# Joined small inputs, an earlier bias, another staging slot and two orders of ScalarE work in a streaming-encoder kernel

## The chip, the cores and the metric

The kernel runs on one core of a Trainium2 chip. The metric is the device time of one execution in microseconds (us). A core has TensorE (PE, whose weight loads are shown as PEld), VectorE (DVE), ScalarE (ACT), GpSimd (POOL) and SyncE (SP). Each engine works through its own queue in order. Transfers are issued from the queues of SP, POOL and ACT and carried out by 16 DMA engines that all queues share.

## The reference

The reference is one step of a two-layer encoder on 1024 prompt frames and 8 streams of 16 sample frames, width 1024, 16 query heads and 4 key/value heads of 64.

```python
# layer 0 (A): windowed attention with ALiBi distances and a learned sink per head
qkv = rmsnorm(x, g_attn[0]) @ w_qkv_a[0]
q = rmsnorm(q, g_q_a[0]); k = rmsnorm(k, g_k_a[0])
x = x + attend(q, k, v, alibi_bias, sink_a[0]) @ w_o_a[0]
x = x + square(relu(rmsnorm(x, g_mlp[0]) @ w_up[0])) @ w_down[0]
# between the layers: shared keys and values
kv = rmsnorm(x, g_kv) @ w_kv;  k = rmsnorm(k, g_k_b)
# layer 1 (B): the last 9 chunks, learned bias on the clipped distance
q = rmsnorm(rmsnorm(x, g_attn[1]) @ w_q_b[0], g_q_b[0])
x = x + attend(q, k, v, relpos_bias(rel_bias_b[0]), None) @ w_o_b[0]
x = x + square(relu(rmsnorm(x, g_mlp[1]) @ w_up[1])) @ w_down[1]
```

The frames are held as nine tiles of 128: eight of the prompt and one, called ST, of all samples.

## The kernel before

Every matmul operand in 32 bits is split into a high part (a cast on ACT, line 128; for scaled attention weights POOL line 185) and a low part (a subtraction on DVE, line 134 or 190), and a product is three matmuls: high by high, high by low, low by high (lines 219 to 221 in `proj`, 745 to 747 in `mm3`).

The stages follow each other: layer 0 attention (about 0 to 400 us), the rest of its output projection (`wo_phase`, to about 442), its up projection (`mlp_up`, to about 798), its down projection (`mlp_down`, to about 1134), and the same four for layer 1.

**Start.** `prep_gains` loads five gain vectors of 1024 with five SP transfers, turns them in one transpose and keeps them as columns. Then come the first token tile, the key/value weights, two more token tiles, and the vectors g_k, g_q (`load_gvec`, line 627), the constants, and the sink in one transfer for all partitions and four for the sample layout (`sinks`, lines 1349 to 1358). `N(t)` makes a token tile ready: `transpose_x` turns it on PE (line 212) and splits it into `hh` and `hl`; `stats` squares it on ACT (line 203) for the norm. `K1` and `Q1` are the key/value and query projections. SP issues in order, so a load that waits for a free buffer holds what stands behind it.

**Up projection.** Sixteen blocks of 256 columns. Each block loads weights on SP (`ru`, line 773), splits them on DVE and ACT and writes squared activations into two tiles of a seven-tile rotation `h`; every second block takes a third. DVE forms sums of them, and POOL stores them to DRAM as `hd` (line 910). A tile of the rotation is free again when its last store has landed.

**Down projection.** Forty items, grouped in chains that add into the same PSUM banks. Item n needs a block `a` of `hd` (loaded on SP into one of three slots, cast on ACT, low part on DVE) and a weight sum `s` or raw weight `r` (added on DVE at line 1062, cast to slot `w0` or `w1` in turn, low part on DVE). After an item, its three banks are copied out (line 1165 ACT to `o` or a token tile, line 1173) or added to a token tile on DVE (line 1177), and POOL transfers add them to DRAM (`xp`/`xd`). The last outputs of layer 0 go, by an ACT copy, into the token tiles x8, x0, x1, from there by line 1168 to DRAM. `DOWN_HOME` is the order of the tiles in memory; layer 1's attention then lays its own tiles over the same addresses, and a tile waits until what lay there before has been read.

**The bias of layer 1's samples.** In the down projection of layer 0, from item 20, `prep_bias` loads the table, fills two tiles on DVE, builds a row per head, and spreads it in DRAM (`rd`, 3 MB); from item 24, `spread_bias` issues sixteen small SP transfers into `big` and one from there to `biasSd`. Their places on DVE and SP are ordered by hand with `behind`.

**Order.** The program order is a priority; a planner with its own estimates of durations fixes each engine's order. `behind(a, b)` puts b after a on the same engine. `chain` orders DVE work in the down projection by hand.

Of the kernel before, what the change touches and what calls it, by code (L numbers as in the profile page):

```python
# [63 lines left out]
C_W = 596  # L64


def shape_constants():
    c = np.zeros((P, C_W), np.float32)
# [19 lines left out]
    return c  # L88

# [5 lines left out]
class Build:  # L95
# [104 lines left out]
    def stats(self, small, junk, x, t):  # L200
        nc = self.nc
        ssq = small.tile([P, 1], F32, tag="xssq", name="xssq")
        nc.scalar.activation(junk, x, AF.Square, accum_out=ssq)
        nc.vector.tensor_scalar(self.vx[:, t : t + 1], ssq, 1.0 / D, EPS, ALU.mult, ALU.add)

    def transpose_x(self, x, hh, hl):
        nc = self.nc
        for half in range(2):
# [4 lines left out]
            self.split(hh[half], hl[half], ps)  # L213
# [753 lines left out]
    def mlp_down(self, layer, out):  # L967
# [3 lines left out]
        with ExitStack() as st:  # L971
# [15 lines left out]
            for n, tags in enumerate(DOWN_HOME):  # L987
                pool = self.pool(st, f"d{n}_{layer}")
                for t in tags.split():
                    if t == "bias":  # L990
                        self.bias_tiles(pool)
                        pool.tile([P, 248], F32, tag="pad", name="pad")
                    elif t[0] == "+":
# [132 lines left out]
            for n, (s, p, g, first, final, reads, _) in enumerate(seq):  # L1126
                if layer == 0 and n == RANK:
                    self.prep_bias(self.dp)
                if layer == 0 and n == RANK + 4:
                    self.spread_bias(self.dp)  # L1130
# [20 lines left out]
                for i in range(3):  # L1151
# [11 lines left out]
                    for o, v in reads:  # L1163
                        if o in adds:
                            nc.scalar.activation(adds[o][i], banks[i], AF.Copy, scale=float(v))  # L1165
# [27 lines left out]
    def bias_tiles(self, pool):  # L1193
        self.tb = pool.tile([H, NREL], F32, tag="tb", name="tb")
        self.fr = pool.tile([H, 384], F32, tag="fr", name="fr")
        self.big = pool.tile([P, KV, 288], F32, tag="big", name="big")

    def prep_bias(self, dp):
        nc = self.nc
        with ExitStack() as st:  # L1200
            tb, fr, big = self.tb, self.fr, self.big
            a = nc.sync.dma_start(tb, self.ins["rel_bias_b"][0])
            self.behind(self.sp, a)
            self.behind(self.dve, nc.vector.memset(fr, 0.0))
            self.behind(self.dve, nc.vector.memset(big, BIG))
            nc.vector.tensor_scalar(
                fr[:, 127:383], tb[:, 256:0:-1], -1.0, tb[:, 256:257], ALU.mult, ALU.add
            )
            fd = dp.tile([H, 384], F32, tag="fd", name="fd")
            nc.sync.dma_start(fd, fr)  # L1210
            rd = dp.tile([H, P, 384], F32, tag="rd", name="rd")
            nc.sync.dma_start(rd, fd[0:H].unsqueeze(1).to_broadcast([H, P, 384]))
            ra = rd[0:H]

            def fsrc(h, off, n, nh, hs, w):
                return bass.AP(
                    tensor=ra.tensor, offset=ra.offset + h * P * 384 + 127 + off,
                    ap=[[383, n], [hs * P * 384, nh], [1, w]],
                )

            self.fsrc = fsrc

    def spread_bias(self, dp):
        nc, big, fsrc = self.nc, self.big, self.fsrc
        for h4 in range(G):
            for b in range(2):
                r = slice(h4 * 32 + b * 16, h4 * 32 + b * 16 + 16)
                c = 256 + b * 16
                for z in (
                    nc.sync.dma_start(big[r, :, b * P : b * P + P], fsrc(h4, 0, 16, KV, G, P)),  # L1230
# [681 lines left out]
```

## Time and profile before

| | us |
|---|---|
| median of 3 runs | 2354.36 (2354.15 to 2357.34) |
| span of the profiled execution | 2349.6 |
| median less span: what lies around it | 4.8 |
| PE busy | 2273.2 |
| DVE busy | 1718.3 |
| ACT busy | 1332.0 |
| POOL busy | 644.7 |

The span runs from the first to the last instruction of one profiled execution; its own time is that span and what lies around it, for which the page has no row; against the median it is 4.8 us. In the timeline a row gives start, length, engine, line, operation, output and inputs, and in square brackets how long the engine was idle before it and what ended the idle time. A row with "x8" merges eight instructions. The mean granted clock of TensorE is 0.993.

### The profile page before, as it was taken

The page shows a single profiled execution, that of the slowest core. Times are in us where ns is not written, and L with a number is a line of the kernel's source. Part 1 is how long each engine was busy: PE and PEld are TensorE (multiplying, and loading weights), DVE is VectorE, ACT ScalarE, POOL GpSimd, SP SyncE. Part 2 cuts the span into 40 slices and gives each one's busy share as a digit, 9 for nine tenths or more (in the row PEclk, how much of TensorE's full clock was granted, in tenths as well). Part 3 has the DMA queues.
Part 4 walks back from the last instruction along what each step waited for, and adds up shares of the span by engine and source line. Part 5 has one row for each costly group of instructions (what it writes and reads, how often), then busy time and mean ns, then how long its engine had stood idle before and what let it go on. Part 6 is the DMA issues. An engine that isn't in the chain of part 4 may idle for free.

```text
span 2349.6 us, 33397 instructions
## 1 busy us (share of the span) xinstructions
PE 2273.2 (97%) x11429; PEld 1899.3 (81%) x11429; DVE 1718.3 (73%) x3075; ACT 1332.0 (57%) x2684; POOL 644.7 (27%) x950
## 2 busy tenths in 40 slices
PE   8999999899999999999899899999899999999999
PEld 6787877788888888778778778887888888888887
DVE  6888786766656578898577776877666566678987
ACT  3777674555555555344377666665655555555443
POOL 4434332313213111002433444345132132210011
PEclk9999999999999999999999999999999999999999
DMA  7435546234334687848654656555243343877567
GB/s 262 128 103 177 166 141 208 89 122 162 132 112 152 218 231 174 272 142 206 191 157 114 190 151 180 166 172 186 72 162 132 114 160 113 276 212 197 183 165 198
DMA packets 226715, 392.70 MB, mean 167 GB/s; under 512 B 51592, under 2 KB 126288, under 8 KB 226448
## 3 DMA queue, kind: packets, MB, share of 16 engines
q1 hardware_dynamic: 188816, 283.58, 37.8%
q0 software_dynamic: 36432, 102.26, 16.0%
q10 hardware_dynamic: 1296, 4.72, 0.5%
q8 instruction: 90, 1.47, 0.3%
q14 instruction: 81, 0.66, 0.1%
HBM read 236.51 MB, written 156.85 MB: 167 GB/s over the span
## 4 chain that ended last, share of the span: by engine, by line
PE 73%; DVE 11%; DMA 8%; ACT 3%; issue 2%; POOL 2%; SPq 1%; ACTq 0%; DVEq 0%; POOLq 0%
PE ps_c L745 7%; PE ps_c L746 7%; PE ps_c L747 7%; PE ps_x L745 5%; PE ps_x L747 5%; PE ps_x L746 5%; PE ps_mm L219 3%; PE ps_mm L221 3%; PE ps_mm L220 3%; PE ps_y L747 2%; PE ps_y L746 2%; PE ps_y L745 2%; PE ps_tr L326 2%; DMA a<-hd 2%; DVE w L134 1%
## 5 line engine op out<-in xcount | busy, mean ns | idle before, releaser
L746 PE MATMUL ps_c<-w,a 128*128 128x512 f32 x960 | 374.0, 390 | 3.9 <-DVE w L134 3.9
L745 PE MATMUL ps_c<-w,a 128*128 128x512 f32 x960 | 374.1, 390 | 3.2 <-ACT o L1165 1.7
L747 PE MATMUL ps_c<-w,a 128*128 128x512 f32 x960 | 373.5, 389 | 0.0
L910 POOL DMA_DIRECT2D hd<-h x272 | 149.4, 552 | 594.3 <-ACT h L819 378.4
L745 PEld LDWEIGHTS ps_c<-w,a 128*128 128x128 f32 x960 | 180.2, 188 | 42.9 <-issue 2.7
L746 PEld LDWEIGHTS ps_c<-w,a 128*128 128x128 f32 x960 | 180.2, 188 | 42.7 <-DVE w L134 5.6
L747 PEld LDWEIGHTS ps_c<-w,a 128*128 128x128 f32 x960 | 180.2, 188 | 37.4
L128 ACT CAST a<-a 128x1536 fp32r<-128x1536 f32 x80 | 118.6, 1483 | 154.6 <-DMA a<-hd 154.6
L219 PE MATMUL ps_mm<-w,hh 128*128 128x512 f32 x432 | 173.9, 403 | 12.8 <-ACT hh L128 5.4
L221 PE MATMUL ps_mm<-w,hl 128*128 128x512 f32 x432 | 172.4, 399 | 1.4 <-DVE hl L134 1.2
L220 PE MATMUL ps_mm<-w,hh 128*128 128x512 f32 x432 | 171.4, 397 | 0.3
L134 DVE TENSOR_TENSOR a<-a 128x1536 fp32r<-128x1536 f32 x80 | 140.6, 1757 | 40.6 <-ACT a L128 40.5
L745 PE MATMUL ps_x<-sx,w 128*128 128x512 f32 (+1 forms) x408 | 157.8, 387 | 4.5 <-ACT h L866 2.7
L128 ACT CAST w<-ru 128x512 fp32r<-128x512 f32 (+1 forms) x160 | 109.9, 708 | 84.4 <-PE ps_y L746 32.0
L128 ACT CAST w<-s 128x2048 fp32r<-128x2048 f32 x56 | 107.1, 1912 | 88.2 <-DVE s L1062 78.8
L747 PE MATMUL ps_x<-sx,w 128*128 128x512 f32 (+1 forms) x408 | 154.2, 378 | 0.3 <-DVE w L134 0.3
L746 PE MATMUL ps_x<-sx,w 128*128 128x512 f32 (+1 forms) x408 | 154.1, 378 | 0.0
L134 DVE TENSOR_TENSOR w<-s,w 128x2048 fp32r<-128x2048 f32 x56 | 128.2, 2289 | 32.3 <-ACT w L128 32.0
L1182 POOL DMA_DIRECT2D xp<-o x28 | 36.2, 1294 | 411.6 <-ACT o L1165 391.0
L134 DVE TENSOR_TENSOR w<-ru,w 128x512 fp32r<-128x512 f32 (+1 forms) x160 | 129.7, 813 | 14.8 <-ACT w L128 14.7
L134 DVE TENSOR_TENSOR ptl<-ps_tr,pth 128x512 fp32r<-128x512 f32 x180 | 122.5, 685 | 21.2 <-ACT pth L128 17.5
L818 ACT ACTIVATE h<-h 128x512 f32<-128x512 f32 (+1 forms) x102 | 61.9, 607 | 122.1 <-DVE h L868 93.0
(274 smaller groups left out, 6152.9 us busy)
## 6 DMA issues: line engine op xcount, KB each, us to landing
a<-hd SPq DMA_DIRECT2D x80, 768.0 KB, 6.2
hd<-h POOLq DMA_DIRECT2D x272, 192.0 KB, 2.5
ru<-in_w_up SPq DMA_DIRECT2D x64, 512.0 KB, 3.9
r<-in_w_down SPq DMA_DIRECT2D x32, 1024.0 KB, 9.8
xp<-o POOLq DMA_DIRECT2D x28, 768.0 KB, 9.5
o<-oTd SPq DMA_DIRECT2D x50, 256.0 KB, 3.9
x<-xp SPq DMA_DIRECT2D x23, 512.0 KB, 5.5
xp<-xo SPq DMA_DIRECT2D x18, 512.0 KB, 2.9
```

The source lines that it names most:

```text
L128: a = nc.scalar.copy(hi, src)
L134: return a, e.tensor_tensor(lo, src, hi.bitcast(F32), ALU.subtract)
L219: nc.tensor.matmul(ps, a, w[:, 0, k, :], start=(k == 0), stop=False)
L220: nc.tensor.matmul(ps, a, w[:, 1, k, :], start=False, stop=False)
L221: self.lp = nc.tensor.matmul(ps, b, w[:, 0, k, :], start=False, stop=(k == KC - 1))
L326: self.lp = nc.tensor.transpose(pt[:, i, :], get(i), self.ident)
L745: a = mm(ps, ah, bh, start=first, stop=False, skip_group_check=True)
L746: mm(ps, ah, bl, start=False, stop=False, skip_group_check=True)
L747: return a, mm(ps, al, bh, start=False, stop=last, skip_group_check=True)
L818: a = nc.scalar.activation(t, src, AF.Relu)
L910: return lambda p, z: self.nc.gpsimd.dma_start(self.hd[c // 4][:, p, c % 4], z)
L1182: nc.gpsimd.dma_start(dst, z, accum_op=ALU.add)
```

## The change

Four edits. (1) The host lays the sinks, g_k and g_q behind the constants in one array of 744 columns and the five gains in one array, so that one transfer loads each; -0.125 is multiplied into g_q in place. (2) The bias preparation moves to the first block of layer 0's up projection. Its tiles are the first two of the seven-tile rotation; its DMAs go to POOL's queue (table, row, sixteen spreads, store), all but the 3 MB spread in DRAM, which stays on SP; no order by hand is given. The addresses that its tiles had in the down projection become a gap. (3) In the last item of a down projection, sums that go straight to DRAM are copied to the weight slot that no later item uses. Only layer 0 has such sums in its last item. (4) In layer 1's attention the square of tiles 0, 1 and ST is ordered behind the casts of that tile, and in both down projections the cast of `a` for item 2 behind the latest copy at line 1165.

```diff
     def stats(self, small, junk, x, t):
-        nc.scalar.activation(junk, x, AF.Square, accum_out=ssq)
+        z = nc.scalar.activation(junk, x, AF.Square, accum_out=ssq)
...
+        return z
...
                 quad, ws = weights(b)
+                if layer == 0 and b == 0:
+                    part, big = [hp.tile([P, 3 * 3 * P], F32, tag="h", name="hb", bufs=7) for _ in range(2)]
+                    self.spread_bias(self.dp, part, big)
...
-                low[n] = [self.split(a[:, 0], a[:, 1], a[:, 1].bitcast(F32))[1]]
+                z = self.split(a[:, 0], a[:, 1], a[:, 1].bitcast(F32))
+                if n == 2:
+                    self.behind(self.copied, z[0])
+                low[n] = [z[1]]
...
-                if layer == 0 and n == RANK:
-                    self.prep_bias(self.dp)
-                if layer == 0 and n == RANK + 4:
-                    self.spread_bias(self.dp)
...
-                            adds[o] = [xs[t][:, N[o % 2]] for t in PARTS[2]]
+                            if n + 1 < total:
+                                adds[o] = [xs[t][:, N[o % 2]] for t in PARTS[2]]
+                            else:
+                                z = take(f"w{(n + 1) % 2}")
+                                adds[o] = [z[:, 0, i].bitcast(F32) for i in range(3)]
                             continue
...
+    def spread_bias(self, dp, part, big):
+        dma = nc.gpsimd.dma_start
+        tb, fr = part[0:H, 0:NREL], part[0:H, 384:768]
+        dma(tb, self.ins["rel_bias_b"][0])
+        nc.vector.memset(fr, 0.0)
+        nc.vector.memset(big, BIG)
+        nc.vector.tensor_scalar(
+            fr[:, 127:383], tb[:, 256:0:-1], -1.0, tb[:, 256:257], ALU.mult, ALU.add
+        )
+        dma(fd, fr)
+        nc.sync.dma_start(rd, fd[0:H].unsqueeze(1).to_broadcast([H, P, 384]))
...
+                dma(big[r, :, b * P : b * P + P], fsrc(h4, 0, 16, KV, G, P))
+                dma(big[r, :, c : c + 16], fsrc(h4, P, 16, KV, G, 16))
+        dma(self.biasSd[0:KV].rearrange("j p c -> p j c"), big)
...
-            for i, v in enumerate(
-                (I["g_attn"][0], I["g_attn"][1], I["g_mlp"][0], I["g_mlp"][1], I["g_kv"])
-            ):
-                nc.sync.dma_start(g[i * KC : (i + 1) * KC, :], v.rearrange("(k p) -> k p", p=P))
+            nc.sync.dma_start(g, I["gains"])
...
-        nc.sync.dma_start(self.sink, I["sink_a"][0].partition_broadcast(P))
+        self.sink = self.cst[:, C_SK : C_SK + H]
...
-        for i in range(G):
-            nc.sync.dma_start(
-                self.ssink[i * 32 : i * 32 + 32, :],
-                sk[i : i + 13 : 4].partition_broadcast(32),
-            )
+        self.ssink = self.cst[:, C_SSK : C_SSK + KV]
...
-                self.transpose_x(x, hh, hl)
-                self.stats(small, self.scratch([P, D], mybir.dt.bfloat16, "junk"), x, t)
+                turned = self.transpose_x(x, hh, hl)
+                z = self.stats(small, self.scratch([P, D], mybir.dt.bfloat16, "junk"), x, t)
+                if not A and t in (0, 1, ST):
+                    self.behind(turned, z)
...
+            if A:
+                self.cst = ring.tile([P, C_W], F32, tag="cst", name="cst")
+                nc.sync.dma_start(self.cst, I["consts"])
+                gk, gq8 = self.cst[:, C_GK : C_GK + HD], self.cst[:, C_GQ : C_GQ + HD]
+                nc.vector.tensor_scalar(gq8, gq8, -0.125, None, ALU.mult)
```

More of the change, by code (lines that the diff above doesn't have):

```diff
@@ L63 @@
 C_SLS = 592
-C_W = 596
+C_SK = 596
+C_SSK = 612
+C_GK = 616
+C_GQ = 680
+C_W = 744
+C_S = 596
 def shape_constants():
-    c = np.zeros((P, C_W), np.float32)
+    c = np.zeros((P, C_S), np.float32)
     q = np.arange(P)[:, None]
@@ L88, in shape_constants, with laid_out @@
     return c
+def laid_out(sink, g_k, g_q):
+    row = np.concatenate([g_k, g_q])
+    return np.concatenate(
+        [
+            shape_constants(),
+            np.broadcast_to(sink, (P, H)),
+            np.repeat(sink.reshape(KV, G).T, P // G, axis=0),
+            np.broadcast_to(row, (P, 2 * HD)),
+        ],
+        axis=1,
+    )
 def halves(t):
@@ L989, in mlp_down @@
                 for t in tags.split():
[L990 to L993, printed above, removed]
+                    if t[0] == "+":
                         pool.tile([P, int(t[1:])], F32, tag="gap", name="gap")
@@ L1164, in mlp_down @@
                         if o in adds:
-                            nc.scalar.activation(adds[o][i], banks[i], AF.Copy, scale=float(v))
+                            self.copied = nc.scalar.activation(
+                                adds[o][i], banks[i], AF.Copy, scale=float(v)
+                            )
                             if o not in whole:
@@ L1396, in attention @@
             ring = self.pool(st, f"ring{layer}")
-            self.pad(st, f"ringpad{layer}", 168 if A else 64)
+            self.pad(st, f"ringpad{layer}", 176 if A else 64)
             apool = self.pool(st, f"att{layer}", 2)
@@ L1875 @@
 ]
+_LAID = ("g_attn", "g_kv", "sink_a", "g_k_a", "g_q_a")
 _OUTS = [
@@ L1896 @@
     given = {n: np.ascontiguousarray(inputs[n]) for n in _INS}
-    given["consts"] = shape_constants()
+    given["consts"] = laid_out(given["sink_a"][0], given["g_k_a"][0], given["g_q_a"][0])
+    given["gains"] = np.concatenate(
+        [given["g_attn"], given["g_mlp"], given["g_kv"][None]]
+    ).reshape(5 * KC, P)
+    for name in _LAID:
+        del given[name]
     given["eye"] = np.eye(P, dtype=np.float32)
```

58 lines of the change are left out of this document (16 added, 42 removed).

## The prediction

> **What bounds the kernel now.** I read the page first, then the chain of waits that ended last, then the waits of PE stage by stage, and last the timelines of all engines around each wait that the change touches.
>
> ```profile
> span 2349.6 us, 33397 instructions
> ...
> PE 2273.2 (97%) x11429; PEld 1899.3 (81%) x11429; DVE 1718.3 (73%) x3075; ACT 1332.0 (57%) x2684; POOL 644.7 (27%) x950
> ```
>
> PE is the bound and the stages stand in series, so an edit is worth the PE idle time that it ends, and 2349.6 - 2273.2 = 76 us of idle time is all there is to win. No edit adds or removes a matmul. The sum is made against the span of 2349.6; the median is 4.8 us more, which I keep as it is.
>
> **Start of layer 0 (edit 1).** Timeline of the first 27 us, SP first, then the engines behind it; the second fence is a row of the chain of waits.
>
> ```profile
> 1.17 0.70 SPq L1246 DMA_DIRECT2D g<-in_g_attn  x2
> ...
> 2.92 0.36 SPq L1426 DMA_DIRECT2D x<-in_x_prompt  x1
> ...
> 9.24 0.33 SPq L1426 DMA_DIRECT2D x<-in_x_sample  x1
> ...
> 10.51 4.38 SPq L1358 DMA_DIRECT2D ssink<-in_sink_a  x4
> ...
> 11.00 0.81 DVE L190 SCALAR_TENSOR_TENSOR w<-raw,gcol,w 128x512 fp32r<-128x512 f32 x1
> ...
> 16.12 0.39 SPq L146 DMA_DIRECT2D raw<-in_w_qkv_a  x1
> ...
> 26.78 0.50 PE L221 MATMUL ps_mm<-w,hl 128*128 128x512 f32 x1 [1.21 <-DVE hl L134]
> ```
> ```profile
> 6.49 9.57 DMA gq<-in_g_q_a
> ```
>
> Five gain loads stand between 1.17 and 2.92, 0.35 us each. Four go, so the first token tile and everything behind it on SP comes 4 x 0.35 = 1.4 us earlier. Of the eight small loads (gk, gq, constants, sink, four ssink) one is left. Today they cost SP 4.38 us for the sinks alone, and the first query weight (16.12) waits until gq has landed, although its buffer was free at 11.0 + 0.81 = 11.8. Afterwards it can go at about 11.8 - 1.4 = 10.4, 5.7 us sooner. PE feels only the last wait: the low part of tile ST stood on DVE behind the low parts of these late weights, 1.21 us. With the weights 5.7 us early that wait goes. Sum 1.4 + 1.2 = **2.6 us**; bounds 0 (the shift ends in a later wait) and 5.7 (the whole advance of the weights).
>
> **Bias moved into the up stage (edit 2).** First what it leaves behind. PE's waits in the middle of the down stage, layer 0, then the same items of layer 1, which has no bias to prepare:
>
> ```profile
> 972.85 0.50 PE L746 MATMUL ps_c<-w,a 128*128 128x512 f32 x1 [1.06 <-DVE w L134]
> 989.75 0.47 PE L745 MATMUL ps_c<-w,a 128*128 128x512 f32 x1 [0.52 <-DVE x L1177]
> ...
> 1000.16 0.50 PE L746 MATMUL ps_c<-w,a 128*128 128x512 f32 x1 [1.74 <-DVE w L134]
> 1017.68 0.50 PE L746 MATMUL ps_c<-w,a 128*128 128x512 f32 x1 [0.91 <-DVE w L134]
> 1034.58 0.47 PE L745 MATMUL ps_c<-w,a 128*128 128x512 f32 x1 [0.51 <-DVE x L1177]
> ```
> ```profile
> 2189.84 0.50 PE L746 MATMUL ps_c<-w,a 128*128 128x512 f32 x1 [0.22 <-DVE w L134]
> 2206.73 0.47 PE L745 MATMUL ps_c<-w,a 128*128 128x512 f32 x1 [0.50 <-DVE x L1177]
> ```
>
> Layer 0 loses 1.06 + 0.52 + 1.74 + 0.91 + 0.51 = 4.74 us, layer 1 0.72. Layer 1 is layer 0 without the bias, so the removal is worth 4.74 - 0.72 = **4.0 us**; bounds 1.06 (only the wait behind the fills of DVE) and 4.74.
>
> Now what it adds. DVE operations and DMAs of the bias, as they are today:
>
> ```profile
> 967.40 0.38 DVE L1204 MEMSET fr<- 16x384 f32 x1
> 967.97 1.02 DVE L1205 MEMSET big<- 128x1152 f32 x1 [0.19 <-issue]
> ...
> 974.92 0.34 DVE L1206 TENSOR_SCALAR fr<-tb 16x256 f32<-16x256 f32 x1
> ```
> ```profile
> rd<-fd SPq DMA_DIRECT2D x1, 3072.0 KB, 15.7
> ...
> biasSd<-big SPq DMA_DIRECT2D x1, 576.0 KB, 5.0
> big<-rd SPq DMA_DIRECT2D x8, 32.0 KB, 5.2
> ...
> fd<-fr SPq DMA_DIRECT2D x1, 24.0 KB, 1.5
> ```
>
> And the place they go to, around the first blocks of the up stage: DVE, POOL, then a stretch (length; busy time and count of PE, PEld, DVE, ACT, POOL; clock; share of the DMA engines; GB/s), and last a group of the page:
>
> ```profile
> 449.20 0.42 DVE L877 TENSOR_TENSOR h<-ps_y,h 128x256 f32<-128x256 f32 x1 [3.99 <-PE ps_y L747]
> ...
> 493.36 0.68 DVE L868 TENSOR_TENSOR h<-ps_z,h 128x512 f32<-128x512 f32 x1
> ```
> ```profile
> 493.74 0.54 POOL L910 DMA_DIRECT2D hd<-ht  x1
> ```
> ```profile
> 446.00:464.00 18.00, 18.00 (x150) 18.00 (x151) 6.31 (x11) 9.90 (x26) 0.60 (x1) 1.00 0.01 1
> ```
> ```profile
> L1182 POOL DMA_DIRECT2D xp<-o x28 | 36.2, 1294 | 411.6 <-ACT o L1165 391.0
> ```
>
> DVE's 0.38 + 1.02 + 0.34 = 1.74 us fit into its idle 3.99 us ahead of 449.2: cost 0. Without that cover, put between the last low parts of the output projection, they would cost their 1.74. In 446 to 464 PE was busy for all of 18.00 us, DVE for 6.31, POOL for 0.60 and the DMA engines for 1%, so this is the emptiest stretch for 3 MB. The chain of the bias: the row is ready at about 445, its store lands by 447.5 (issue 0.54, landing 1.5), the 3 MB by 463 (15.7, measured under full load), sixteen spreads on POOL at 0.54 to 1.29 each by 472 to 484, their landing 5.2 and the store to `biasSd` 5.0 by 483 to 495. Who waits for that: the two bias tiles are the first two of the rotation and come round in block 2, whose second product is added at 493.36; its first copy stands 1.7 us ahead of that and the first write of the second tile, `big`, about 1.1 us behind, at some 494.5. So even the dear end only touches it: cost **0**, bound -1.7. Behind the spreads on POOL stand the first `hd` stores (from 463 on); they end some 10 to 20 us later, and their tiles are wanted in block 3, 22 us after block 2. On SP the weight loads of the next blocks stand behind the 3 MB issue, which waits until the row has landed (447.5); those weights are first cast at 458.
>
> [...]
>
> **First copies of the down stage (edit 4, second half).** Layer 0, then layer 1:
>
> ```profile
> 807.88 0.50 PE L745 MATMUL ps_c<-w,a 128*128 128x512 f32 x1 [1.38 <-ACT o L1165]
> ```
> ```profile
> 2025.85 0.50 PE L745 MATMUL ps_c<-w,a 128*128 128x512 f32 x1 [0.28 <-ACT o L1165]
> ```
>
> Item 1 adds into banks that must first be copied, and the copies stood on ACT behind the cast of `a` for item 2. Put ahead of it, they end with item 0's matmuls: 1.38 + 0.28 = **1.7 us**. The cast is then late by three copies, but item 2 starts a whole item (8 us) later. Bounds 0 and 1.7.
>
> **From layer 0 to layer 1 (edits 3 and 4).** ACT, POOL, PE and SP here:
>
> ```profile
> 1132.16 1.06 ACT L203 ACTIVATE junk<-x 128x1024 bf16<-128x1024 f32 x1 [1.35 <-DMA x<-xp]
> ...
> 1140.13 1.07 ACT L128 CAST hh<-ps_n 128x512 fp32r<-128x512 f32 x2 [5.84 <-DMA xp<-x]
> ```
> ```profile
> 1134.16 1.77 POOL L1168 DMA_DIRECT2D xp<-x  x2
> ```
> ```profile
> 1134.34 1.09 PE L212 MATMUL ps_n<-identr,x 128*128 128x128 f32 x8 [0.67 <-ACT x L1165]
> 1140.86 0.76 PE L219 MATMUL ps_mm<-w,hh 128*128 128x512 f32 x1 [5.43 <-ACT hh L128]
> ...
> 1145.42 0.40 PE L221 MATMUL ps_mm<-w,hl 128*128 128x512 f32 x1
> 1145.66 0.40 PE L219 MATMUL ps_mm<-w,hh 128*128 128x512 f32 x1
> ```
> ```profile
> 1133.74 0.38 SPq L146 DMA_DIRECT2D raw<-in_w_q_b  x1
> ```
>
> This is the largest term. The cast of `hh` does not wait for data: it waits for the transfer `xp<-x` that reads the last sums from token tiles lying at the addresses of `hh`. With the sums in slot w0, far from `hh`, the cast can follow the transposes, and PE's 5.43 us go. The 0.67 us go too: the square at 1132.16 stood ahead of the last copies. There is a third part: eleven matmuls fill 1140.86 to 1145.42, 0.41 us each, against 0.24 after (1145.42 to 1145.66), so the wait also cost 11 x 0.17 = 1.9 us of slow matmuls. [...] Together 5.43 + 0.67 + 1.9 = 8.0 us.
>
> Against it stands a new wait. The first query weight (1133.74) lands in the buffer of token tile 0, which the square must have read. That square now follows the casts: ACT ends its copies at about 1133.4, two casts make it 1134.5, square and read-out 1.25 more, so the load goes at 1135.8, 2.1 us later than today, while PE wants it 8 us sooner. I take those 2.1 us off: **5.9 us**; bounds 0 (the weights give the pace) and 8.0.
>
> **Sum.** 2.6 + 4.0 + 1.7 + 5.9 = 14.2 us. Span 2335.4, time 2354.4 - 14.2 = **2340.2 us**.
>
> **The rivals.**
>
> *The query weights take over.* What the transition wins is lost again at layer 1's first query projection, whose weights pass through two buffers. For it speaks the later first load, against it that SP, too, was held by the stalled cast. Then 2.6 + 4.0 + 1.7 = 8.3 and 2346.1 us.
>
> *The bias was not what held the down stage.* DVE is full in that stretch, and the waits move to other sums. For it: two of five waits end with `x L1177`, which layer 1 has as well. Against it: layer 1's 0.72. Then 14.2 - 4.0 = 10.2 and 2344.2 us.
>
> *Slower: POOL cannot clear the spreads before block 2.* Place: the copy into `big`, at 494.5. If each spread costs not 0.54 to 1.29 but a landing of 5.2 us, sixteen take 83, `big` is free at 463 + 83 + 5 = 551, and PE stands for 56 us: 2340.2 + 56 = 2396 us. It decides from the spread at which the stall eats the 14.2: 463 + 16 s + 10.2 = 494.5 + 14.2, s = 2.2 us. Against it: no POOL issue in the groups is that dear.
>
> *It does not do what it says.* The order of all else comes from the planner, which is fed with changed loads at the start and may give a few us away in either attention stage; if it gives away most of the sum, 2351 or more.
>
> **Chances.** Forecast 0.56; query weights 0.18; bias 0.14; nothing measurable 0.07; slower 0.05. A measurement of this kernel tells 0.2% (4.7 us) from no change: faster is below 2349.7. Faster 0.88, same 0.07, slower 0.05. The range: 2334, from the upper bounds (5.7 + 4.74 + 1.7 + 8.0 = 20.1), to 2350, the lower bounds of two of the large terms at once.
>
> **What would show it.** First query load near 10.4 and no wait of PE near 25; no DVE fills in the down stage and its PE waits near layer 1's 0.7; no wait of item 1; the first `hh` of layer 1 straight behind the transposes, matmuls at 0.23 from the start. Wrong would be: a PE wait in block 2 or 3 of the up stage, or a wait for query weights of over 3 us in layer 1's start.

## The result, and the profile after

The changed kernel takes 2342.06 us (median of 5 runs, 2339.97 to 2346.06), the kernel before 2354.36 beside it: 0.9944 of the time, 95% interval 0.9928 to 0.9959 (the ratio on record; the two medians alone give 0.9948). Measured once more beside the last experiment it was 0.9958 (0.9945 to 0.9971). The profiled execution has a span of 2340.3 us, 1.8 less than its time; for every later execution, also of the kernel before, that difference is 1.8. If the profile of before is no exception, only 1.8 of the 4.8 us that the prediction carried over between span and median lie around the span, and its profiled execution was 3.0 us shorter than the median of its runs; the two profiles differ by 9.3 us where the medians differ by 12.3.

First the heads of the page after:

```profile
span 2340.3 us, 33405 instructions
...
PE 2270.6 (97%) x11429; PEld 1897.5 (81%) x11429; DVE 1719.7 (73%) x3075; ACT 1332.7 (57%) x2684; POOL 653.6 (28%) x969
```

PE does the same work; its idle time fell from 76 to 70 us. To place the gain I aligned PE's instructions of two traces in order and took, at a few of them, the start in the profile before less the start in the other. This lead is positive where the other kernel is ahead; what it gains in a stage is a gain of that stage. The place called 1150 is read at 1167: the kernels order the matmuls from 1141 to 1167 differently, and there they have done the same ones again.

| instruction, by its time before | changed | changed, again | forecast |
|---|---|---|---|
| 61, first projection behind the first key read-out | +2.9 | +1.0 | +2.6 |
| 169, sample probabilities turned | -2.3 | -5.9 | +2.6 |
| 450, up stage under way | -4.3 | -5.2 | +2.6 |
| 950, down stage, ahead of the bias | -2.9 | -3.3 | +4.3 |
| 1050, behind the bias | +2.7 | +1.9 | +8.3 |
| 1150, layer 1's first projections | +5.1 | +4.9 | +14.2 |
| 1400, layer 1 attention | +7.5 | +8.2 | +14.2 |
| 2330, end | +9.5 | +10.6 | +14.2 |

**Layer 0.** SP's start, then PE at 80, in the timeline of the changed kernel:

```profile
1.18 0.40 SPq L1257 DMA_DIRECT2D g<-in_gains  x1
1.63 0.36 SPq L1427 DMA_DIRECT2D x<-in_x_prompt  x1
...
8.87 0.34 SPq L1427 DMA_DIRECT2D x<-in_x_sample  x1
...
14.24 0.55 SPq L164 DMA_DIRECT2D raw<-in_w_qkv_a  x1
```
```profile
80.44 0.38 PE L402 MATMUL ps_s<-KT,qT 128*128 128x256 f32 x1 [1.32 <-ACT p L417]
83.33 0.98 PE L402 MATMUL ps_s<-KT,qT 128*128 128x256 f32 x3 [2.50 <-DMA KT<-KT]
84.10 0.63 PE L239 MATMUL ps_mm<-w,hh 128*128 128x512 f32 x1
...
87.94 0.50 PE L239 MATMUL ps_mm<-w,hh 128*128 128x512 f32 x1
```

The first token tile is asked for 1.3 us earlier (1.63 for 2.92), the PE wait of 1.21 at 26.78 is gone. Then comes something new: four scores stand on PE ahead of the next projection, where before the projection came first, and wait 1.32 and 2.50 us; the nine matmuls behind them start 0.43 apart instead of 0.23. That is 3.8 + 9 x 0.2 = 5.6 us at one place.

**Up stage.** PE at its start, and the bias on POOL, in the timeline:

```profile
442.09 1.97 PE L712 MATMUL ps_n<-identr,s 128*128 128x128 f32 x8 [1.22 <-DVE sx L152]
446.93 0.58 PE L765 MATMUL ps_x<-sx,w 128*128 128x256 f32 x1 [1.16 <-ACT h L886]
```

```profile
450.64 0.50 POOL L1229 DMA_DIRECT2D fd<-hb  x1 [4.01 <-DVE hb L1225]
466.12 0.53 POOL L1246 DMA_DIRECT2D hb<-rd  x1 [14.98 <-ACT w L146]
...
474.69 0.57 POOL L933 DMA_DIRECT2D hd<-h  x1
...
477.73 0.78 POOL L1249 DMA_DIRECT2D biasSd<-hb  x1
```

Sixteen spreads at 0.51 to 0.53 us each are issued by 474.7; no PE wait follows in blocks 2 and 3.

**Down stage.** The stretch with the bias in one row each, before and after (length; busy time and count of PE, PEld, DVE, ACT, POOL; clock; DMA share; GB/s):

```profile
960.00:1040.00 80.00, 75.26 (x327) 60.71 (x327) 70.19 (x59) 32.99 (x22) 0.00 (x0) 1.00 0.59 193
```
```profile
960.00:1040.00 80.00, 79.70 (x352) 65.66 (x352) 74.13 (x58) 34.71 (x25) 0.00 (x0) 1.00 0.45 153
```

PE gets 352 matmuls done where it did 327. The only PE wait left in layer 0's down stage is 0.30 us at 991.11; the wait of item 1 is gone too.

**Layer 0 to layer 1.** PE, then SP, then DVE of the changed kernel:

```profile
1133.25 3.31 PE L231 MATMUL ps_n<-identr,x 128*128 128x128 f32 x16 [3.14 <-DMA x<-xp]
1136.31 0.48 PE L239 MATMUL ps_mm<-w,hh 128*128 128x512 f32 x1
1136.63 0.40 PE L240 MATMUL ps_mm<-w,hh 128*128 128x512 f32 x1
1138.20 0.66 PE L231 MATMUL ps_n<-identr,x 128*128 128x128 f32 x4 [1.17 <-DVE hl L152]
```
```profile
1115.36 0.34 SPq L1427 DMA_DIRECT2D x<-xp  x1
...
1124.56 0.34 SPq L647 DMA_DIRECT2D gk<-in_g_k_b  x1
1124.95 0.42 SPq L647 DMA_DIRECT2D gq<-in_g_q_b  x1
1125.43 0.42 SPq L1630 DMA_DIRECT2D biasB<-rd  x1
1126.02 1.43 SPq L1427 DMA_DIRECT2D x<-xp  x2
```
```profile
1137.25 0.29 DVE L580 TENSOR_TENSOR kc<-kc,gq 128x128 f32<-128x128 f32 x1 [4.95 <-DMA kc<-in_cache_k_b]
1137.46 1.28 DVE L152 TENSOR_TENSOR hl<-ps_n,hh 128x512 fp32r<-128x512 f32 x2
```

The cast of `hh` no longer waits for `xp<-x`, and the projection runs at 0.23 from its first matmuls. The slow matmuls are not all gone, though: the sixteen transposes ahead of it take 3.31 us, where before the last eight take 1.09. And the token tiles themselves are late (3.14), and then the low parts (1.17), because DVE stands at a product with gq and waits for cached keys.

### The profile page after: what moved, and what is told of

The parts are those of the page before. It is cut to its first block, busy times and chain, and to the rows that moved or that the text cites. A ratio compares the mean times of both kernels' runs of the same rounds, so it can differ in the third digit from the quotient of the medians.

```text
span 2340.3 us, 33405 instructions
## 1 busy us (share of the span) xinstructions
PE 2270.6 (97%) x11429; PEld 1897.5 (81%) x11429; DVE 1719.7 (73%) x3075; ACT 1332.7 (57%) x2684; POOL 653.6 (28%) x969
## 4 chain that ended last, share of the span: by engine, by line
PE 76%; DVE 9%; DMA 6%; issue 4%; ACT 3%; POOL 1%; SPq 0%; POOLq 0%; ACTq 0%; DVEq 0%
PE ps_c L765 7%; PE ps_c L767 7%; PE ps_c L766 7%; PE ps_x L765 5%; PE ps_x L766 5%; PE ps_x L767 5%; PE ps_mm L239 4%; PE ps_mm L241 4%; PE ps_mm L240 4%; PE ps_y L767 2%; PE ps_y L766 2%; PE ps_y L765 2%; PE ps_tr L346 2%; PE ps_mm L194 2%; PE ps_mm L195 1%
```

## The experiments

All times are ratios to the kernel before on the same chip, with the 95% interval. The table has the leads of each run's profile over the profile of before at the places of the table above. Lines differ by a few between the kernels.

| run | ratio | 61 | 169 | 450 | 950 | 1050 | 1150 | 1400 | end |
|---|---|---|---|---|---|---|---|---|---|
| inputs undone | 0.9953 (0.9935 to 0.9971) | -1.1 | -1.1 | -1.5 | 0.0 | +6.2 | +10.3 | +11.0 | +12.7 |
| bias undone | 0.9998 (0.9984 to 1.0012) | +3.1 | -1.9 | -7.1 | -6.2 | -6.8 | -4.2 | -3.8 | -2.1 |
| squares undone | 0.9955 (0.9938 to 0.9973) | +3.3 | -1.8 | -3.6 | -1.8 | +4.1 | +4.7 | +3.9 | +7.6 |
| slot undone | 0.9958 (0.9943 to 0.9972) | +3.6 | -0.8 | -2.8 | -1.5 | +4.7 | +8.5 | +5.0 | +7.8 |
| bias alone | 0.9964 (0.9950 to 0.9979) | -1.7 | -1.7 | -2.9 | -3.2 | +2.5 | +2.2 | +1.9 | +1.5 |
| tiles first on SP | 0.9957 (0.9945 to 0.9968) | +3.1 | -1.9 | -3.9 | -2.6 | +3.1 | +3.8 | +2.2 | +3.7 |
| tiles, keys' product later | 0.9953 (0.9936 to 0.9970) | +2.8 | -2.3 | -1.8 | -0.5 | +5.1 | +6.3 | +6.0 | +7.8 |
| tiles, all small work later | 0.9945 (0.9927 to 0.9963) | +1.0 | -5.8 | -8.1 | -6.5 | -0.7 | +6.9 | +5.0 | +5.3 |
| scores later on PE | 0.9979 (0.9964 to 0.9994) | +3.4 | -0.8 | -12.0 | -10.6 | -5.1 | -3.9 | -3.8 | 0.0 |
| keys first on ACT | 0.9979 (0.9965 to 0.9992) | +3.0 | -1.3 | -10.5 | -9.1 | -3.3 | -1.0 | -1.7 | +0.1 |
| combination | 0.9948 (0.9935 to 0.9960) | 0.0 | 0.0 | -4.4 | -3.0 | +2.3 | +10.5 | +6.6 | +5.0 |
| changed, again | 0.9958 (0.9945 to 0.9971) | +1.0 | -5.9 | -5.2 | -3.3 | +1.9 | +4.9 | +8.2 | +10.6 |

### One part undone at a time

Each kernel is the changed one with one part put back. The four expectations in the order inputs, bias, squares, slot:

```diff
 inputs undone
-                nc.sync.dma_start(g, I["gains"])
+            for i, v in enumerate(
...
+                nc.sync.dma_start(g[i * KC : (i + 1) * KC, :], v.rearrange("(k p) -> k p", p=P))
 bias undone
-                    self.spread_bias(self.dp, part, big)
+                if layer == 0 and n == RANK:
+                    self.prep_bias(self.dp)
+                if layer == 0 and n == RANK + 4:
+                    self.spread_bias(self.dp)
 squares undone
-                if not A and t in (0, 1, ST):
-                    self.behind(turned, z)
 slot undone
-                                z = take(f"w{(n + 1) % 2}")
-                                adds[o] = [z[:, 0, i].bitcast(F32) for i in range(3)]
+                            adds[o] = [xs[t][:, N[o % 2]] for t in PARTS[2]]
```

The constants, sinks, gk and gq are loaded as before where the inputs are undone. The spans of the four are 2338.1, 2352.5, 2342.2 and 2342.2.

> The changed kernel with the small inputs loaded as before (edit 1 undone). My theory: edit 1 wins 2.8 us by 60 us, but the changed loads at the start also changed the planner's order of the matmuls near 80 us, where scores now stand ahead of a projection and wait for a key copy; that costs about 5 us. Without edit 1 the wait near 83 us (2.50 us) is gone and the first block of the up stage starts about 2.3 us earlier than in the changed kernel: span 2338, against 2340.3. Rival: the wait has another cause (the bias, or chance of timing); then it stays and only the start is lost: span 2343.

> The changed kernel with the bias prepared in the down stage as before (edit 2 undone). My theory: the down stage of layer 0 gets back PE waits of about 4 us (1.06, 1.74, 0.91 and smaller ones), the up stage starts about 1 us sooner because the two fills no longer stand among the last low parts: span 2343. Rival, the waits of the down stage come from elsewhere: they do not return, span 2340 or less. A second rival: the bias, early at hand, is what let its load go ahead of the token tiles at layer 1's start; then that wait of 3.14 us goes as well and the span stays near 2340 although the down stage is 4 us longer.

> The changed kernel without the order of layer 1's first squares behind the casts. My theory: token tile 0 arrives late there (1133 us), so the square goes ahead of the casts and puts them 1.2 us off per tile: span longer by 1 to 2.5 us, 2342. Rival: PE waits for the tiles and the low parts anyway, and ACT has the time: same span.

> The changed kernel with layer 0's last sums staged in the token tiles again (edit 3 undone). My theory: the first cast of layer 1 waits for the last of three transfers out of x8, x0, x1, which ends near 1140.5, instead of 1134.4: span longer by 4 to 6 us, 2345, and the first matmuls slow. Rival: the token tiles' late loads would have held the stage anyway, and most of the slot's worth is not there: longer by less than 2 us.

*Bias.* This is the part that carries the result: without it the ratio is 0.9998. Its five waits are all back and sum to 1.23 + 0.48 + 2.21 + 0.91 + 0.52 = 5.35 us. PE's waits in the down stage of the kernel with the bias undone:

```profile
979.26 0.50 PE L766 MATMUL ps_c<-w,a 128*128 128x512 f32 x1 [1.23 <-DVE w L152]
996.16 0.47 PE L765 MATMUL ps_c<-w,a 128*128 128x512 f32 x1 [0.48 <-DVE x L1206]
1007.01 0.50 PE L766 MATMUL ps_c<-w,a 128*128 128x512 f32 x1 [2.21 <-DVE w L152]
1024.53 0.50 PE L766 MATMUL ps_c<-w,a 128*128 128x512 f32 x1 [0.91 <-DVE w L152]
1041.44 0.47 PE L765 MATMUL ps_c<-w,a 128*128 128x512 f32 x1 [0.52 <-DVE x L1206]
```

Between 950 and 1050 this kernel loses 0.6 us where the changed one gains 5.6. Its span was expected at 2343 and came out at 2352.5: of the 11.6 us that separate it from the changed kernel at the end, the down stage's bias has 6.2; 2.8 more are lost before 450 and 2.3 behind 1150, which the theory didn't have. The second rival fell: PE waits 3.03 us for x at layer 1's start in this kernel too. Its trace also tells what the fills cost at the start of the up stage, where DVE runs them between the last low parts of the output projection: nothing. With them PE goes from its last transposes to the next product in 446.93 - 442.09 = 4.84 us, without them in 449.59 - 444.75 = 4.84. The same two instructions of the kernel with the bias undone:

```profile
444.75 1.97 PE L712 MATMUL ps_n<-identr,s 128*128 128x128 f32 x8 [1.45 <-DVE sx L152]
449.59 0.58 PE L765 MATMUL ps_x<-sx,w 128*128 128x256 f32 x1 [1.16 <-ACT h L886]
```

The kernel before, without fills there, and the bias alone, with them, say the same: 4.18 and 4.19 us.

*Inputs.* The ratio can't be told from that of the changed kernel. The trace says where the 2.6 us went: without the joined inputs PE's order in layer 0 is that of before, row for row, there is no wait at 80, and at 169 this kernel is 1.2 us ahead of the changed one although it started 3.9 us behind.

*Squares and slot.* Neither ratio can be told from the changed kernel's. By stages, the order of the squares is worth 2.4 - 0.6 = 1.8 us between 1050 and 1150, the slot nothing there: without it the lead grows by 3.8. The expected 4 to 6 us didn't come. The first reason is on ACT. Without the slot the cast of `hh` does wait for `xp<-x` again, but for 1.87 us and not 5.84 (6.33 with the bias alone, where the squares stand as before), and PE for 1.48 and not 5.43. ACT of that kernel:

```profile
1128.18 0.60 ACT L1184 ACTIVATE x<-ps_c 128x512 f32<-128x512 f32 x1 [2.12 <-PE ps_c L767]
1130.64 1.08 ACT L146 CAST hh<-ps_n 128x512 fp32r<-128x512 f32 x2 [1.87 <-DMA xp<-x]
```

With the squares behind the casts each of the last sums is copied when PE has it, and the three transfers are issued at 1123.63, 1126.42 and 1129.22. Before, the squares waited for token tiles ahead of these copies, and one transfer went at 1131.14 and two at 1134.16. So the order of the squares alone takes away most of the wait that the prediction gave to the slot. A second wait took part of the win here: PE waits 1.45 us at 1145.08 for a query weight, and POOL, which prepares it, waits for its load; that is the prediction's first rival.

The second reason is on SP. Its order at the layer's start without the slot:

```profile
1119.77 2.77 SPq L1423 DMA_DIRECT2D x<-xp  x2
1132.64 0.67 SPq L1423 DMA_DIRECT2D x<-xp  x1
1133.40 1.02 SPq L647 DMA_DIRECT2D gk<-in_g_k_b  x1
```

Here, as before, two token tiles are loaded first, and a third (ST, which the program loads last) behind them with gk and gq. With the slot the group of the one tile and these vectors goes ahead: in the changed kernel one tile at 1115.36, gk, gq and a bias tile from 1124.56, and the other two last, at 1126.02. That order holds in every kernel with the slot whose SP order I did not turn by hand, and in none without it.

### The bias alone

The kernel before, with the new `spread_bias` in the up stage and without the bias tiles and the two calls in the down stage:

```diff
+                if layer == 0 and b == 0:
+                    part, big = [hp.tile([P, 3 * 3 * P], F32, tag="h", name="hb", bufs=7) for _ in range(2)]
+                    self.spread_bias(self.dp, part, big)
...
-                if layer == 0 and n == RANK:
-                    self.prep_bias(self.dp)
-                if layer == 0 and n == RANK + 4:
-                    self.spread_bias(self.dp)
```

> The kernel before with one part of the change: the bias is prepared in the up stage. Theory (the move takes DVE and SP work out of the down stage, and nothing in the up stage waits for it): the five PE waits of 4.74 us between 972 and 1035 fall to about 0.3, the wait of item 1 (1.38 us) stays, the up stage starts where it started before (first matmul behind the 1.74 us wait at 443.7, within 1 us), and the lead at the end of the down stage is the 5.6 us by which the changed kernel pulls ahead there beyond item 1: span 2349.6 - 5.6 = 2344. Rival 1 (the fills on DVE hold up the start of the up stage): 2.5 us are lost between 425 and 450, span 2346.5. Rival 2 (the bias is worth what undoing it cost, 2352.5 - 2340.3 = 12.2): span 2337.5.

The gain between 950 and 1050 is 5.7 us, the wait of item 1 stays (1.45), the other five fall to one of 0.26. The span is 2348.4 and not 2344, since this execution had already lost 2.9 us up to 450, 1.7 of them in the first 61 us, where PE's order is row for row that of before. By the ratio the part is worth 5 to 12 us. The first theory stands; the second rival's 12.2 isn't excluded by the ratio, but no stage shows it.

### The token tiles first

In the first run SP's loads of gk and gq (`load_gvec`) and of the bias tile (`bias_b`) stand behind the load of token tile 1. In the second, DVE's first products with gq stand behind the low parts of that tile as well, and in the third also the scaling of gq and the fill of `biasB`. The expectations call all of these loads small; gk and gq have 32 KB, but the bias tile has 512 KB like a token tile.

```diff
 first, second and third
+        self.behind(self.xls[1], z)
 second and third
+        if layer and j == 0 and bp < 2:
+            self.behind(self.first_low, z)
 third
+            self.behind(self.first_low, z)
...
+                if j < 2:
+                    self.behind(self.first_low, z)
```

> The changed kernel with SP's order turned at layer 1's start: the two gain vectors (gk, gq) and the bias loads stand behind the load of token tile 1, where they stood ahead of both token tiles. Theory (these small loads delay the token tiles, which landed 7 us after their issue): the PE wait of 3.14 us for x falls to at most 1, the gain shows at the first projection of layer 1; the wait for low parts (1.17) may grow to 2, since gq then lands later and DVE's product with gq stands ahead of them; span 2338.3 (2340.3 less 2). Rival (the token tiles wait for their own data, the sums accumulated in memory): the wait stays at 2.5 us or more, span 2340.3 or more.

> As the kernel with the token tiles first on SP, and in addition DVE's first products of the cached keys with gq stand behind the low parts of token tile 1. Theory (small loads delay the token tiles, and the product with gq delays the low parts): both waits go, 3.14 to at most 1 and 1.17 to at most 0.3; span 2340.3 - 3 = 2337.3. Rival (tiles wait for their data): span 2340 with the wait of 3.14 kept; if only the second part holds, 2339.

> The changed kernel with layer 1's first token tiles first on SP and with all of DVE's operations on the small loads (the scaling of gq, the fills of biasB, the products with gq) behind the low parts of token tile 1. Theory (what held the transition were small loads that land 6 to 10 us after their issue, first as SP's predecessors of the token tiles and then, with the tiles first, as DVE's predecessors of the low parts: 4.98 and 4.82 us of PE wait in the two runs that moved only a part): no PE wait over 1 us between the first transposes and the first read-out of layer 1, matmuls at 0.23 from the start, a lead at the first transposes of layer 1 that is about 3.1 + 1.2 us over the changed kernel at 1150; span 2336. Rival (the query weights or the keys' cache give the pace next): a new PE wait of 3 us or more before 1200, span 2340 or more.

The first half of the theory holds at once: the wait of 3.14 us for x is gone in all three. But in the first two a wait of 4.98 and of 4.82 us stands in its place, for the low parts. PE of the second run, then its DVE:

```profile
1134.77 1.12 PE L231 MATMUL ps_n<-identr,x 128*128 128x128 f32 x4 [4.82 <-DVE hl L152]
```
```profile
1129.99 0.20 DVE L653 TENSOR_SCALAR gq<-gq 128x64 f32<-128x64 f32 x1 [7.65 <-DMA gq<-in_g_q_b]
...
1133.90 0.27 DVE L1640 MEMSET biasB<- 64x256 f32 x1 [3.45 <-DMA biasB<-rd]
1134.09 1.22 DVE L152 TENSOR_TENSOR hl<-ps_n,hh 128x512 fp32r<-128x512 f32 x2
```

DVE works in order, so a fill of 0.27 us that waits for a transfer holds 1.2 us of low parts that everything else waits for. With all of this behind the low parts PE has no wait of 0.3 us or more between 1100 and 1173, and the lead grows by 7.5 us from 1050 to 1150, against 2.4 in the changed kernel: more than the 5.9 of the prediction. At 1400 the growth is down to 5.6, and the changed kernel, which had 2.4, has 4.9 by then. The next PE wait, 2.97 us at 1173.95 for qT (2.24 before), comes near what the rival named, and slow transposes follow it. The span was 2344.6, since this execution was 8.1 us behind at 450; the ratio is that of the changed kernel. So the transition is mended, and in this profile most of it isn't kept.

### The order at 80

In the first run the first score of group (2, 0) stands on PE behind the projection's matmuls, which are also written ahead of it. In the second, two exponentials and the copy `pvt` stand on ACT behind token 3's second read-out of kw:

```diff
 scores later
+                    early = A and g == 2 and i == 1
+                    if early:
+                        fill(i)
...
+                        if (t, j) == (2, 0) and i == 0 and v == 0:
+                            self.behind(self.lproj, z)
 keys first
+        if t == 3 and self.held is not None:
+            for y in self.held.values():
+                self.behind(z, y)
```

> The changed kernel with one order changed in layer 0: the scores of the second token group stand behind the next projection's matmuls on PE, as they stood before the change (the planner had put four scores ahead of them, where they wait 1.32 us for p and 2.50 us for KT, and nine matmuls behind them ran at 0.43 us each). Theory (the start's 2.6 us is won and lost again in that one order): no PE wait between 79 and 86, all matmuls there at 0.23, a lead of about 5 us over the changed kernel at 171, kept to the end: span 2335.3, ratio near 0.9925. Rival 1 (the wait for KT moves on to the next consumer): lead below 2, span 2338.5 or more. Rival 2 (the other choices of the planner give it away by the start of the up stage): lead of 5 at 171 but below 2 at 450.

> The changed kernel with one order changed on ACT in layer 0: the read-out of token 3's keys (kw, 2 operations) stands ahead of two exponentials and the copy pvt, where the planner had put it behind them; with that alone the planner puts the projection's matmuls ahead of the scores again, as before the change. Theory (the 5 us lost between 79 and 89 come from that late read-out, which holds the projection's accumulator: where the scores stood first they waited for KT, and where the projection stood first it waited 3.79 us for kw): no PE wait over 1 us between 75 and 95, matmuls at 0.23, and at 171 a lead of 4 to 5.5 us over the changed kernel; if the rest of layer 0 keeps it, span 2335.5. Rival (another operand is late as well, KT or qT): a wait of 2 us or more appears within 10 us of that place and the lead at 171 is below 2: span 2339 or more.

In the first run the wait moved to the next consumer: the projection stood first and waited for its accumulator, which ACT reads out (kw) only behind other work. So in the second run that read-out was moved up. PE of both:

```profile
82.44 0.50 PE L239 MATMUL ps_mm<-w,hh 128*128 128x512 f32 x1 [3.79 <-ACT kw L306]
```
```profile
81.12 0.80 PE L239 MATMUL ps_mm<-w,hh 128*128 128x512 f32 x1 [2.04 <-ACT kw L306]
```

It still waits 2.04 us, and at 169 the two are 1.4 and 1.0 us ahead of the changed kernel, not 5. The sizes are those of the rivals (a lead below 2). But the operand of the second run is still kw: on ACT the casts of qT and `pth` (79.32 and 79.92) stand ahead of its read-out (80.40). So of the 5.6 us, these two orders win about one; that no other order wins more isn't shown. And by their ratio, 0.9979, both kernels are 5 to 8 us slower than the changed one (their intervals stand apart from that of its first measurement and overlap that of its second): between 169 and 450 they lose 11 and 9 us against the kernel before, the changed one 2. The edits touch one place near 80, but PE's order then differs from the changed kernel's in many places from 213 on, in the same way in both, and most of the loss falls in the output projection, between 340 and 385. PE in the output projection of the run with the scores later, at its new waits:

```profile
349.79 0.58 PE L194 MATMUL ps_mm<-w,oh 128*128 128x512 f32 x1 [2.00 <-DVE xo L1628]
...
374.25 0.80 PE L194 MATMUL ps_mm<-w,oh 128*128 128x512 f32 x1 [1.84 <-DVE xo L1628]
```

### The combination, and the changed kernel again

The combination is the changed kernel with the inputs as before and the third of the orders for the token tiles.

> The changed kernel with the small inputs as before (the first part of the change undone) and with layer 1's token tiles and their low parts first, as in the run that moved all of DVE's operations on the small loads. Theory (losses add up: the input arrays' order costs about 3 us in layer 0's plan by the profiles, the transition's waits about 1 us net): about 3 us below the changed kernel on the same chip, ratio near 0.993. Rival 1 (executions of one kernel differ by several us in layer 0, and the profile that spoke for the old inputs was a fast one): no difference from the changed kernel beyond 1.5 us, ratio 0.994 to 0.996. Rival 2 (what the transition wins is given back in layer 1): the lead at 1150 is over 12 us against the kernel before, and under 10 at the end.

> The changed kernel once more, unaltered, beside the combination on the same chip. By the result: ratio 0.9944, within 0.9928 to 0.9959. By its stages: the same order of instructions, so the same waits at 80 and 83 and at layer 1's start; the start of the up stage within 3 us of the first profile if executions differ by slow matmuls alone.

The combination takes 2342.37 us, the changed kernel beside it 2344.77; the ratios 0.9948 and 0.9958 overlap, so it isn't shown to be better; 0.9948 lies where the first rival put it. Its profile has the second rival's pattern, though the number in it (over 12 at 1150) was not reached: the lead is 10.5 at 1150 and 5.0 at the end. The 8.2 us that it wins from 1050 to 1150 shrink by 3.9 until 1400, and 2.3 of these go at one place, layer 1's first sample scores. PE there in the combination, then the same eight transposes in the kernel before:

```profile
1170.30 0.89 PE L440 MATMUL ps_sn<-KT,qT 128*128 128x128 f32 x6 [2.90 <-DVE qT L138]
1171.02 1.79 PE L217 MATMUL ps_n<-identr,x 128*128 128x128 f32 x8
```
```profile
1180.80 1.06 PE L212 MATMUL ps_n<-identr,x 128*128 128x128 f32 x8
```

The wait is 0.7 us longer than the 2.24 of before, and what follows runs slowly: 1.6 us more, at a granted clock of 0.70 from 1170 to 1175.6 where before had 1.00. The same 1.6 us are lost here in seven of the thirteen later profiles, five of them behind a wait of 2.24 to 2.49, and in neither of the two of the changed kernel. The other 1.6 us of the 3.9 I did not settle.

## Why the prediction came out right, and where its steps failed

The time lies 1.9 us from the forecast, inside the range, and faster is what was likeliest. The steps are less good than that: by the profiles the sum of 14.2 is 9.5 to 10.6, and the terms are not where they were put. The 3.0 us by which the profile before was short hid part of the difference. And errors cancel: in the first profile layer 0 up to 450 ends 6.9 us short of its term and the transition 3.5, while the bias gives 1.6 more than its own and layer 1 has 4.4 that were not forecast. So that the sum came near is luck in part.

**Start, 2.6.** The start itself came as forecast: +2.9 at 61, the wait at 26.78 gone. Two details were wrong. The first query load went at 14.24 and not near 10.4: SP issues in order, and the sample tile (8.87) and stores of `hh` and `hl` stand ahead of it. And the gain ended in a later wait, the case for which the lower bound of this term, 0, was made; it fell below it. Over the eight profiles with the joined inputs and no hand in layer 0's order the lead at 169 is -2.8 on average, over the four with the old inputs (before itself among them) -0.7; at 450 -4.6 and -2.2. So by the profiles, which scatter by 6, this part cost about 2 us instead of winning 2.6; the ratios can't tell it from nothing. The prediction had this as the last rival: the planner, fed with changed loads, gives a few us away.

**Bias out of the down stage, 4.0.** Right mechanism, size too small: 5.6, 5.2 and 5.7 us (changed, again, alone), above its upper bound of 4.74. The term was mis-sized in two ways. Layer 1's 0.72 was taken off as what would remain; 0.26 to 0.51 remained. And the idle time in a row's brackets isn't all that a wait costs: 25 more matmuls in the same 80 us are 25 x 0.227 = 5.7 us, where the idle time fell by 4.4. The first matmul behind each wait takes 0.50 against 0.39. The rival by which the bias was not what held the stage is excluded by the run that undid it.

**Bias in the up stage, 0.** Right, though not as argued. The fills did not use DVE's idle 3.99 us; they stood between the last low parts of the output projection, the very place that the prediction priced at 1.74, and cost nothing, since PE's interval there is the same with and without them (4.84 us in one pair of kernels, 4.19 and 4.18 in the other). The spreads took the low end of their price. The slow rival needed 2.2 us for each; they took 0.53 at most, with VectorE at work beside them for 6.06 of the 8.60 us from 466.1 to 474.7.

**First copies, 1.7.** Right: 4.34 - 2.66 = 1.7 at item 2, of which 1.4 are kept at 950.

**Transition, 5.9.** What was to go went: the cast waits for nothing, the 0.67 is gone, the matmuls run at 0.23 (the slow ones are now transposes, about 1.1 us). That the wait cost the 1.9 us of slow matmuls was an estimate, and no run shows the wait as their cause: the granted clock is 0.51 from 1138.2 to 1145.0 before, and 0.50 from 1132.6 to 1136.0 in the changed kernel. The step that failed is the new wait: it wasn't the query weights' load but the token tiles' (3.14) and the low parts (1.17), and the term gave 2.4 to 3.0. Part of it could be read off before. The square at 1132.16 had waited for its tile until then; with PE done 2.5 us earlier, that tile was due to be next. What could not be read off is that the free slot would turn SP's order, so that the tile came 1 us later still instead of earlier. The rival that names query weights had the right shape and the wrong load; only without the slot were they what PE waited for. And the 5.43 us were put to the slot alone: without it only 1.48 of them come back, since the squares had held the copies from which `xp<-x` starts.

**Layer 1, 0.** From 1150 to the end the changed kernel gains 4.4 and 5.7 us that nobody forecast. Most of that is TensorE's clock. In stretches of 3.4 us, or twice that, the traces show half the clock granted (0.50 from 1646.9 to 1653.7 before). Behind 1167 the profile before has four times 3.4 us of it (at 1308.9 and 1336.2, and 6.8 us at 1646.9), the changed kernel two (6.8 us at 1637.8), and again one (1641.9). One such place, before and changed, in the columns of the stretches above:

```profile
1300.00:1345.00 45.00, 38.98 (x193) 32.32 (x192) 35.33 (x84) 25.95 (x68) 17.66 (x21) 0.92 0.58 182
```
```profile
1300.00:1345.00 45.00, 39.27 (x211) 31.65 (x210) 39.97 (x100) 30.37 (x81) 20.45 (x24) 1.00 0.67 208
```

What ran in these stretches without a wait took 5.8 us longer than the same matmuls and transposes elsewhere, against 2.4 and 1.7 in the changed kernel's two profiles: by this estimate 3.4 of the 4.4 and 4.1 of the 5.7. Over all fourteen profiles it is 1.6 to 8.2 us, with no order by kernel that I can see, so this part of the gain is luck as far as these profiles tell. In the two kernels with the mended transition the same stretch loses 1.6 and 5.5 us. By the same estimate slow matmuls give 1.2 us back in the first and take 2.4 in the second, and the rest, about 3 in each, is waiting; what sets these waits stays open.

Taken together, transition and layer 1 give 6.8 and 8.7 against the 5.9 forecast; without the squares' order 3.5, without the slot 3.2, with neither (bias alone) -1.0. With the slow matmuls behind 1167 counted as in the profile before, these are 3.4 and 4.6, then 2.9, 3.9 and -3.7. So one of the two parts seems to be worth as much as both; that both are needed isn't shown.

## What to carry to other kernels

Where a planner fixes the order, an edit is paid twice: once at its place, and once where the planner orders other work differently because of it. Before a wait is priced at zero, look up in each in-order queue what will be due next, and whether anything small that waits for a transfer stands ahead of it. And with executions of one kernel 6 us apart, compare stages over several profiles, not the ends of two, and look at the granted clock of a stretch before a gain there is put to an edit.

## What the runs showed that I had not expected

The two profiles of the changed kernel have the same order of instructions and the same wait of 1.75 us near 50, and yet the second loses 1.6 us more behind it (49.82 less 49.52 ahead, 60.05 less 58.19 at the next read-out). First the one, then the other:

```profile
49.52 0.66 PE L282 MATMUL ps_q<-identr,qr 128*128 128x128 f32 x4 [1.75 <-DVE qr L261]
...
51.52 0.40 PE L240 MATMUL ps_mm<-w,hh 128*128 128x512 f32 x1
```
```profile
49.82 0.66 PE L282 MATMUL ps_q<-identr,qr 128*128 128x128 f32 x4 [1.75 <-DVE qr L261]
...
51.85 0.63 PE L239 MATMUL ps_mm<-w,hh 128*128 128x512 f32 x1
```

And the granted clock of the same stretch in both, in the columns of the stretches above:

```profile
49.00:59.00 10.00, 8.48 (x44) 6.98 (x45) 8.13 (x25) 6.39 (x17) 1.64 (x4) 1.00 0.59 194
```
```profile
49.00:59.00 10.00, 9.04 (x40) 7.50 (x40) 6.56 (x15) 5.39 (x11) 1.93 (x3) 0.83 0.60 192
```

In the second, seven matmuls from 51.25 on are 0.42 us or more apart, and they begin 1.4 us after PE had work again. Between 49 and 110 us that execution has 25 such matmuls, the first 9. So the same wait, with what runs slowly behind it, comes to 1.75 us or 3.35. What decides between the two these rows do not show: the gap ahead is 1.75 us in both, and the granted clock behind it 1.00 in the first and 0.83 in the second.
